# A hybrid decoder layer (differential attention and gated linear attention): the order of every engine's instructions made by a list scheduler over tiles

## The chip, the cores and the metric

The kernel runs on all 8 cores of one Trainium2 chip, each with one sequence of the batch. The time is that of the slowest core, in microseconds of the device. Executions come in two states. In the slow one the cores of one die (0 to 3 or 4 to 7) show a lower granted TensorE clock: in one execution of the kernel before, of 2403 us, cores 4 to 7 ran at 0.742 to 0.744 and cores 0 to 3 at 0.847 to 0.850. Names of engines in the profile: PE is TensorE's matmul, PEld its weight load, DVE is VectorE, ACT is ScalarE, POOL is GpSimd, SP is the queue that issues DMAs.

## The reference

Each sequence of 4096 tokens of width 1024 goes through this (cut to what matters):

```python
h = rms_norm(x, g_pre)
proj = h @ w_in                                   # (B, S, 5648)
qa, ka, va, za, qb, kb, vb, zb, lr, gate_a, gate_b = split(proj)
# mixer A: 4 heads, two score maps each, causal, ALiBi
pd = softmax(qa1 @ ka1.T * scale + bias) - lam * softmax(qa2 @ ka2.T * scale + bias)
oa = rms_norm(pd @ va, g_sub_a) * (1.0 - lam_init)
ya = (oa * silu(za)) @ w_up_a
# mixer B: gated linear attention (GLA), a chunked recurrence over the sequence
ob = rms_norm(gla_chunked(qb, kb, vb, glog), g_sub_b)
yb = (ob * silu(zb)) @ w_up_b
# merge, output projection, post-norm, residual
y = sigmoid(gate_a) * ya + sigmoid(gate_b) * yb
out = x + rms_norm(y @ w_out, g_post)
```

## The kernel before

A core works through 8 tiles of 512 tokens. Weights are converted to bf16 in the first tile, written to a scratch in HBM, and streamed from there in chunks of 1 MB for the later tiles. A small recorder collects operations with what they read and write. Each engine then runs its operations in the order written, with waits where data cross engines. The overlap of stages is therefore what the author wrote into the order by hand:

```python
        for t in range(ntiles):
            # [cut: norm of the first tile, first weight loads, debug stops]
            phase_b1(t)              # GLA projections
            gla_at(t, 0)
            gla_rest(t, 0)
            phase_b2(t)              # Q, K, V and silu(z_a) projections
            # [cut: the deferred pieces of GLA and of the norm of attention's output]
            for s in range(4):
                attention_jobs(t, s, deferred)
                # [cut: refill deferred]
            # [cut: load and statistics of the next tile's input]
            phase_e(t, lambda: attn_post(t))     # gates, up-projections, merge
            # [cut: hooks that put the next tile's norm between the steps of phase_f]
            phase_f(t, hooks)                    # output projection, post-norm, residual
```

Within attention, scores for one key block go out ahead of the value products of the block before, and pieces of GLA come in at four fixed places:

```python
        def attention_jobs(t, h, deferred):
            nkb = 4 * t + 4
            # [cut: emit_qk_pair issues two 64-row score matmuls of 512 queries, mask matmuls on
            #  the diagonal, and one exponential of 128x1024 on ScalarE; emit_pv issues up to four
            #  value products of 129 columns for one map]
            for kb in range(nkb + 1):
                if kb < nkb:
                    emit_qk_pair(kb)
                if kb >= 1:
                    emit_pv(kb - 1, 0)
                    emit_pv(kb - 1, 1)
                    r_done = (kb - 1) - 4 * t
                    if r_done >= 1:
                        attention_evac(t, h, r_done)
                # [cut: tile 0]
                else:
                    for f in deferred.get(kb, ()):
                        f()
```

In PSUM the program lays out 4 banks for projections and scores alike, 1 for transposes and 3 for the attention accumulators. The normalized input (hT), the queries, and the buffers of the merge exist once; several share memory (silu of z lies in the merge's output, the attention output's transpose in the queries).

Of the kernel before, what the change touches and what calls it, by code (L numbers as in the profile page):

```python
# [10 lines left out]
F32 = mybir.dt.float32  # L11
# [6 lines left out]
D = 1024  # L18
# [6 lines left out]
C_QA, C_KA, C_VA, C_ZA, C_QB, C_KB, C_VB, C_ZB, C_LR, C_GA, C_GB = 0, 512, 1024, 1536, 2048, 2304, 2560, 3072, 3584, 3600, 4624  # L25
CHUNK_COL = [C_QA, C_KA, C_VA, C_ZA, C_QB, C_VB, C_ZB, C_GA, C_GA + 512, C_GB, C_GB + 512]
CH_QA, CH_KA, CH_VA, CH_ZA, CH_QK, CH_VB, CH_ZB, CH_GA0, CH_GA1, CH_GB0, CH_GB1, CH_WO0, CH_WO1 = range(13)
NEG = -30000.0
NSLOT = 4

ENGS = ("pe", "act", "dve", "pool", "sp")

class _Op:
    __slots__ = ("eng", "fn", "deps", "is_dma", "sem", "val", "needs_inc")

    def __init__(self, eng, fn, is_dma):
        self.eng = eng
        self.fn = fn
        self.deps = []
        self.is_dma = is_dma  # L40
        self.sem = None
        self.val = 0
        self.needs_inc = is_dma

class _Prog:
    def __init__(self, same_eng_sync=("act", "dve", "pool")):
        self.ops = []
        self.last_writer = {}
        self.readers = {}
        self.same_eng_sync = set(same_eng_sync)  # L50
        self.dma_slots = []

    def op(self, eng, fn, reads=(), writes=(), dma=None):
        o = _Op(eng, fn, dma is not None)
        deps = {}
        for k in reads:
            w = self.last_writer.get(k)
            if w is not None:
                deps[id(w)] = w
        for k in writes:  # L60
            w = self.last_writer.get(k)
            if w is not None:
                deps[id(w)] = w
            for r in self.readers.get(k, ()):
                deps[id(r)] = r
        o.deps = list(deps.values())
        for k in reads:
            self.readers.setdefault(k, []).append(o)
        for k in writes:
            self.last_writer[k] = o  # L70
            self.readers[k] = []
        if dma is not None:
            o.sem = dma
            if dma not in self.dma_slots:
                self.dma_slots.append(dma)
        self.ops.append(o)
        return o

    def emit(self, block_engines, sems):
        ops = self.ops  # L80
        for o in ops:
            for d in o.deps:
                if d.is_dma:
                    continue
                if d.eng != o.eng or (d.eng in self.same_eng_sync):
                    d.needs_inc = True
        cnt = {e: 0 for e in ENGS}
        dcnt = {}
        for o in ops:
            if o.is_dma:  # L90
                slot = o.sem
                dcnt[slot] = dcnt.get(slot, 0) + 16
                o.sem = sems[slot]
                o.val = dcnt[slot]
            elif o.needs_inc:
                cnt[o.eng] += 1
                o.sem = sems[o.eng]
                o.val = cnt[o.eng]
        same = self.same_eng_sync

        def make(eng_name):
            my_ops = [o for o in ops if o.eng == eng_name]

            def body(e):
                waited = {}
                for o in my_ops:
                    need = {}
                    for d in o.deps:
                        if (not d.is_dma) and d.eng == eng_name and eng_name not in same:
                            continue  # L110
# [17 lines left out]
def _build(ntiles=NT, debug=False, stop_after=None):  # L128
    nc = bass.Bass("TRN2", target_bir_lowering=False)
# [6 lines left out]
    w_up_a = din("w_up_a", [512, D])  # L136
    w_up_b = din("w_up_b", [512, D])
# [7 lines left out]
    negm_d = din("negmask", [128, 128], BF16)  # L145
    btab_d = din("biastab", [128, 128])
    ef_d = din("eftab", [128, 4])
    rmask_d = din("resetmask", [128, 512], BF16)
    out = nc.dram_tensor("out", [S, D], F32, kind="ExternalOutput").ap()
    wsc = nc.dram_tensor("wsc", [13, 128, 4096], BF16).ap()  # L150
    dbg = {}
    if debug:
        for nm, shp in (("d_hT", [128, 8, 512]), ("d_QT", [128, 4, 512]), ("d_oacc", [128, 4, 4, 128]),
                        ("d_ob", [128, 4, 512]), ("d_yT", [128, 8, 512]), ("d_gaT", [128, 4, 512]),
                        ("d_gbT", [128, 4, 512]),
                        ("d_eb", [128, 2, 512]), ("d_state", [128, 2, 128])):
            dbg[nm] = nc.dram_tensor(nm, shp, F32, kind="ExternalOutput").ap()

    P = _Prog()
    with ExitStack() as es:  # L160
# [3 lines left out]
        def PSM(name, shape, dt):  # L164
# [3 lines left out]
        V = SB("V", [128, 4 * ntiles, 4, 130], BF16)  # L168
        wupA = SB("wupA", [128, 4, 1024], BF16)
        wupB = SB("wupB", [128, 4, 1024], BF16)  # L170
        wbuf = [SB(f"wbuf{i}", [128, 4096], BF16) for i in range(NSLOT)]
        wlr = SB("wlr", [128, 8, 16], BF16)
        walpha = SB("walpha", [16, 256], BF16)
        xn = [SB(f"xn{i}", [128, 1024], F32) for i in range(2)]
        xr = xn
        xa = [SB(f"xa{i}", [128, 1024], F32) for i in range(2)]
        hb = [SB(f"hb{i}", [128, 1024], BF16) for i in range(2)]
        hT = SB("hT", [128, 8, T], BF16)
        gated = [hb[i][:, 0:512] for i in range(2)]
        obf = [hb[i][:, 512:1024] for i in range(2)]  # L180
        QT = SB("QT", [128, 4, T], BF16)
        yT = SB("yT", [128, 8, T], BF16)
        szA = yT[:, 0:4, :]
        szB = yT[:, 4:8, :]
        gbT = SB("gbT", [128, 4, T], BF16)
        gl = SB("gl", [128, 2, T], F32)
        sq = gl[:, 0, :]
        lamv = gl[:, 0, 0:256]
        lamt = gl[:, 0, 256:384]
        wlr_st = gl[:, 1, 0:128].rearrange("p (kc c) -> p kc c", kc=8)  # L190
        cum = SB("cum", [128, 2, T], F32)
        walpha_st = cum[0:16, 0, 0:256]
        enb = cum
# [3 lines left out]
        vb = SB("vb", [128, 4, 512], BF16)  # L197
        lrT = SB("lrT", [16, T], BF16)
        state = SB("state", [128, 2, 128], F32)
        stbf = SB("stbf", [128, 2, 128], BF16)  # L200
        PT2 = [SB(f"PT{i}", [128, 2, 512], BF16) for i in range(2)]
        gatedA = SB("gatedA", [128, 4, 512], BF16)
        khT = gatedA[:, 0:2, :]
        oaf = [SB(f"oaf{i}", [128, 128], F32) for i in range(4)]
        junkb = SB("junkb", [128, 128], BF16)
        otmp = [SB(f"otmp{i}", [128, 128], F32) for i in range(2)]
        gaT = QT
        eb = SB("eb", [128, 2, T], F32)
        tga = [eb[:, 0, :], eb[:, 1, :]]
        ttmp = tga  # L210
        ztmp = [PT2[i][:].rearrange("p a b -> p (a b)").bitcast(F32) for i in range(2)]
        eblast = SB("eblast", [128, 2, 4], F32)
        tgb = [SB("tgb0", [128, 512], F32)] * 2
        ATs = [SB("ATs0", [128, 512], BF16)] * 2
        ident = SB("ident", [128, 128], BF16)
        tri4 = SB("tri4", [128, 512], BF16)
        negm = SB("negm", [128, 128], BF16)
        btab = SB("btab", [128, 128], F32)
        eft = SB("eft", [128, 4], F32)
        rmask = SB("rmask", [128, 512], BF16)  # L220
        gpost = SB("gpost", [128, D], F32)
        smalls = SB("smalls", [128, 12], F32)
        lams = SB("lams", [128, 8], F32)
        nbal = SB("nbal", [128, 2], F32)
        ss = SB("ss", [128, 32], F32)
        rs = SB("rs", [128, 32], F32)
        rstd = SB("rstd", [128, 32], F32)
        ssa = SB("ssa", [128, 16], F32)
        rsa = SB("rsa", [128, 16], F32)
        rstda = SB("rstda", [128, 16], F32)  # L230
        ssb = SB("ssb", [128, 16], F32)
        rsb = SB("rsb", [128, 16], F32)
        rstdb = SB("rstdb", [128, 16], F32)
        ssz = SB("ssz", [128, 64], F32)
        rsz = SB("rsz", [128, 32], F32)
        rstdz = SB("rstdz", [128, 32], F32)
        rz = SB("rz", [128, 8], F32)
        dbgbuf = SB("dbgbuf", [128, 8, 512], F32) if debug else None
        dbgoa = SB("dbgoa", [128, 4, 4, 128], F32) if debug else None
        pg4 = PSM("pg4", [128, 4, 512], F32)  # L240
        pg = [pg4[:, i, :] for i in range(4)]
        ptr = PSM("ptr", [128, 8, 128], BF16)
        poa = [PSM(f"poa{i}", [128, 512], F32) for i in range(3)]

        dma_names = (["stg%d" % i for i in range(8)] + ["wst%d" % i for i in range(NSLOT)] + ["wld%d" % i for i in range(NSLOT)]
                     + ["cst", "xn0", "xn1", "xr0", "xr1", "xa0", "xa1", "st0", "st1", "dbg"])
        sems = {}
        for nm in list(ENGS) + dma_names:
            sems[nm] = es.enter_context(nc.semaphore("s_" + nm))
        _build.sbuf_left = nc.sbuf_bytes_remaining  # L250
        block = es.enter_context(nc.Block())

        gctr = [0]

        def alloc_pg():
            b = gctr[0] % 4
            gctr[0] += 1
            return b

        def wkeys(slot):  # L260
            return [f"w{slot}_{i}" for i in range(8)]

        def ev_engine(i):
            return "dve"
# [87 lines left out]
        def emit_load():  # L352
            i = wstate["loaded"]
            if i >= len(wseq):
                return
# [661 lines left out]
```

## Time and profile before

| | before |
|---|---|
| median (3 fast runs) | 2246.97 us, 2242.42 the lowest |
| cores | 2225.9 to 2247.1 us, clock 0.842 to 0.851 |
| TensorE busy, idle (core 4) | 1704.0 us, 543 us |
| ScalarE, VectorE busy | 843.7 us, 934.1 us |
| granted clock (core 4) | 0.846 |

A row of the profile such as `L703 PE MATMUL ps_poa<-sb_V,sb_PT ... x4224 | 396.8, 244 | 123.3 <-ACT ...` reads: line of the program, engine, operation, written tile and read tiles, count, busy time in us, mean ns of one, idle time of the engine just before such instructions, and what ended it. In the rows of 40 slices each digit is tenths of a slice. The recorded lengths of successive matmuls overlap, so the mean of 393 ns for 512 columns is not their spacing, which is about 216 ns in dense stretches. The lines themselves are shown in the prediction.

### The profile page before, as it was taken

The numbers are of one execution on the slowest core, as the hardware profiler recorded it, in microseconds if no ns is written. First come the engines' busy times: TensorE is split into PE (matmuls) and PEld (weight loads), VectorE is DVE, ScalarE is ACT, GpSimd is POOL, SyncE is SP. The second block draws the span as 40 slices with busy tenths as digits, with TensorE's granted clock in tenths as the row PEclk, the third lists the DMA queues.
The fourth block names the chain that finished last, engine by engine and source line by source line (L and its number), as shares of the span: only waits on it lengthen the run. The fifth ranks groups of instructions, "written<-read, shape, count | busy, mean of one in ns | idle before, by whom it ended". The sixth has DMA issues, their size and how long they took to land.

```text
span 2247.1 us, 32959 instructions; the slowest of 8 cores (2225.9 to 2247.1 us)
## 1 busy us (share of the span) xinstructions
PE 1704.0 (76%) x10609; PEld 868.4 (39%) x10704; DVE 934.1 (42%) x2699; ACT 843.7 (38%) x1109; POOL 235.6 (10%) x438
## 2 busy tenths in 40 slices
PE   2554669787977877887878878778787878787786
PEld 1222324443444334443444434444334443344443
DVE  2446445544544454334523454323452234422324
ACT  2321221322144224523166232663316652256642
POOL 1002110111012001101001010010100010000100
PEclk9675789678977987798898988989898989899898
DMA  7992152104310341015300243000530003410002
GB/s 193 261 274 79 50 184 106 55 35 173 112 39 1 133 150 75 1 38 187 131 1 1 77 169 111 1 1 38 188 132 1 1 1 132 150 57 1 1 1 113
DMA packets 48615, 194.10 MB, mean 86 GB/s; under 512 B 6832, under 2 KB 7360, under 8 KB 35136
## 3 DMA queue, kind: packets, MB, share of 16 engines
q1 hardware_dynamic: 41968, 161.59, 21.6%
q0 software_dynamic: 6480, 30.41, 3.6%
q8 instruction: 89, 1.46, 0.3%
q14 instruction: 78, 0.64, 0.1%
HBM read 161.57 MB, written 30.41 MB: 85 GB/s over the span
## 4 chain that ended last, share of the span: by engine, by line
PE 55%; DVE 15%; ACT 9%; issue 9%; DMA 6%; POOL 4%; SPq 1%; DVEq 1%; ACTq 0%; POOLq 0%
PE ps_pg L399 16%; PE ps_pg L407 9%; PE ps_poa L703 9%; ACT sb_PT L694 8%; PE ps_pg L676 4%; DMA sb_KT<-w_in 3%; PE ps_pg L823 3%; PE ps_pg L831 3%; PE ps_pg L866 2%; POOL sb_rstda L772 2%; POOL sb_rstdb L429 2%; PE ps_poa L866 2%; DVE sb_junkb L765 2%; PE ps_pg L684 2%; PE ps_pg L688 2%
## 5 line engine op out<-in xcount | busy, mean ns | idle before, releaser
L694 ACT ACTIVATE sb_PT<-ps_pg 128x1024 bf16<-128x1024 f32 (+1 forms) x576 | 540.7, 953 | 428.3 <-PE ps_pg L676 238.6
L703 PE MATMUL ps_poa<-sb_V,sb_PT 128*128 128x129 bf16 x4224 | 396.8, 244 | 123.3 <-ACT sb_PT L694 93.4
L399 PE MATMUL ps_pg<-sb_hT,sb_wbuf 128*128 128x512 bf16 x1743 | 415.7, 393 | 20.6 <-ACT sb_eb L814 11.4
L703 PEld LDWEIGHTS ps_poa<-sb_V,sb_PT 128*128 128x128 bf16 x4224 | 291.2, 108 | 283.5 <-issue 277.7
L399 PEld LDWEIGHTS ps_pg<-sb_hT,sb_wbuf 128*128 128x128 bf16 x1792 | 180.4, 101 | 243.1 <-issue 52.4
L407 PE MATMUL ps_pg<-sb_wbuf,sb_hT 128*128 128x512 bf16 x994 | 239.4, 399 | 6.6 <-DVE sb_V L559 2.1
L676 PE MATMUL ps_pg<-sb_QT,sb_KT 64*128 64x512 bf16 x896 | 205.3, 448 | 21.0 <-DVE sb_yT L571 9.8
L731 DVE RECIPROCAL sb_rz<-ps_poa 128x3 f32<-128x3 f32 (+1 forms) x96 | 16.4, 171 | 481.5 <-PE ps_poa L703 481.5
L407 PEld LDWEIGHTS ps_pg<-sb_wbuf,sb_hT 128*128 128x128 bf16 x1024 | 103.8, 102 | 139.1 <-issue 36.5
L453 PE MATMUL ps_ptr<-sb_ident,sb_hb 128*128 128x128 bf16 x256 | 28.7, 281 | 129.0 <-DVE sb_hb L448 129.0
L814 ACT ACTIVATE sb_eb<-ps_pg 128x512 f32<-128x512 f32 x64 | 38.2, 597 | 234.2 <-PE ps_pg L399 234.2
L569 ACT ACTIVATE sb_PT<-ps_pg 128x512 f32<-128x512 f32 x32 | 19.0, 596 | 277.4 <-PE ps_pg L407 271.5
L826 DVE SCALAR_TENSOR_TENSOR sb_gl<-sb_eb,ps_pg 128x512 f32<-128x512 f32 x64 | 44.0, 688 | 177.2 <-PE ps_pg L823 163.9
L613 POOL CAST sb_stbf<-sb_state 128x128 bf16<-128x128 f32 x64 | 18.8, 294 | 888.5 <-PE ps_pg L597 694.9
L772 POOL TENSOR_TENSOR sb_rstda<-sb_rsa,sb_lams 128x1 f32<-128x1 f32 x128 | 69.7, 567 | 395.2 <-DVE sb_rsa L770 395.2
L645 PE MATMUL ps_ptr<-sb_ident,sb_hb 128*128 128x128 bf16 x128 | 18.0, 290 | 87.0 <-DVE sb_hb L636 87.0
L866 PE MATMUL ps_pg<-sb_wbuf,sb_yT 128*128 128x512 bf16 x320 | 76.1, 390 | 2.4 <-DVE sb_yT L837 2.4
L676 PEld LDWEIGHTS ps_pg<-sb_QT,sb_KT 64*128 64x128 bf16 x896 | 43.9, 95 | 85.6 <-issue 55.6
L453 PEld LDWEIGHTS ps_ptr<-sb_ident,sb_hb 128*128 128x128 bf16 x256 | 22.0, 126 | 139.3 <-issue 139.3
L823 PE MATMUL ps_pg<-sb_QT,sb_wupA 128*128 128x512 bf16 x248 | 70.7, 410 | 6.7 <-DVE sb_QT L789 6.3
L880 POOL TENSOR_TENSOR sb_rstdz<-sb_rsz,sb_lams 128x1 f32<-128x1 f32 x32 | 27.9, 873 | 429.6 <-DVE sb_rsz L878 429.6
L831 PE MATMUL ps_pg<-sb_gbT,sb_wupB 128*128 128x512 bf16 x256 | 72.2, 408 | 0.0
(116 smaller groups left out, 1932.2 us busy)
## 6 DMA issues: line engine op xcount, KB each, us to landing
sb_wbuf<-wsc SPq DMA_DIRECT2D x91, 1024.0 KB, 4.9
sb_KT<-w_in SPq DMA_DIRECT2D x88, 256.0 KB, 8.8
sb_xa<-x SPq DMA_DIRECT2D x32, 512.0 KB, 6.2
sb_xn<-x SPq DMA_DIRECT2D x32, 512.0 KB, 6.3
out<-sb_xn POOLq DMA_DIRECT2D x32, 512.0 KB, 5.4
wsc<-sb_wbuf POOLq DMA_DIRECT2D x13, 1024.0 KB, 9.9
sb_KT<-w_out SPq DMA_DIRECT2D x16, 256.0 KB, 8.5
sb_KT<-w_up_a SPq DMA_DIRECT2D x8, 256.0 KB, 10.0
```

The source lines that it names most:

```text
L399: P.op("pe", lambda e, lhsT=lhsT, kc=kc: e.matmul(out=pg[b][0:rows, :], lhsT=lhsT, rhs=hT[:, kc, :], start=(kc == 0), stop=(kc == 7)), rea ...
L407: P.op("pe", lambda e, kc=kc: e.matmul(out=pg[b][:, :], lhsT=hT[:, kc, s * 128:(s + 1) * 128], rhs=wbuf[slot][:, kc * 512:(kc + 1) * 512], ...
L429: P.op("pool", lambda e, q_=q_: e.tensor_tensor(out=dst[:, col0 + q_:col0 + q_ + 1], in0=src[:, col0 + q_:col0 + q_ + 1], in1=lams[:, 5:6] ...
L453: P.op("pe", lambda e, kc=kc: e.transpose(out=ptr[:, kc, :], in_=hb[i][:, kc * 128:(kc + 1) * 128], identity=ident[:]), reads=[f"hbL{i}", ...
L676: P.op("pe", lambda e, b=b, lhsT=lhsT, m=m: e.matmul(out=pg[b][:, :], lhsT=lhsT, rhs=QT[64 * m:64 * m + 64, h, :], start=True, stop=True), ...
L684: P.op("pe", lambda e, b=b: e.matmul(out=pg[b][:, c0:c0 + 128], lhsT=ident[:, :], rhs=negm[:, :], start=False, stop=True), reads=["ident", ...
L694: P.op("act", lambda e: e.activation(out=PT2[pp][:, :, c0:512], in_=pg4[:, bp:bp + 2, c0:512], func=AF.Exp, bias=cbias, scale=1.0), reads= ...
L703: P.op("pe", lambda e, a=a, i_=i_: e.matmul(out=acc_ap(m, a, 0, 129), lhsT=PT2[pp][:, m, a * 128:(a + 1) * 128], rhs=V[:, kb, h, 0:129], s ...
L772: P.op("pool", lambda e, ci=ci: e.tensor_tensor(out=rstda[:, ci:ci + 1], in0=rsa[:, ci:ci + 1], in1=lams[:, 5:6], op=ALU.pow), reads=[f"rs ...
L823: P.op("pe", lambda e, kc=kc, j=j, bya=bya: e.matmul(out=pg[bya][:, :], lhsT=wupA[:, kc, j * 128:(j + 1) * 128], rhs=gaT[:, kc, :], start= ...
L831: P.op("pe", lambda e, kc=kc, j=j, byb=byb: e.matmul(out=pg[byb][:, :], lhsT=wupB[:, kc, j * 128:(j + 1) * 128], rhs=gbT[:, kc, :], start= ...
L866: P.op("pe", lambda e, kc=kc, kk=kk, slw=slw, hh=hh, zb_=zb_: e.matmul(out=zb_, lhsT=yT[:, kc, s * 128:(s + 1) * 128], rhs=wbuf[slw][:, kk ...
```

## The change

The intent: at every moment, run on TensorE whatever is ready, from whichever stage and tile. The recorder becomes a list scheduler that runs when the program is built. Each operation carries an estimated cost and the engines that can do it (a copy may go to VectorE or ScalarE). The scheduler repeatedly places the operation that can start first; among equal starts, the one of the lower priority number, then the one written first. Buffers are given out from pools as operations are placed. The core of the diff (about 1,700 lines in all; cuts marked):

```diff
+SEM_LAT = 0.14
+ATT, PRE, GLA, FILL = 0, 1, 2, 3
...
+    def schedule(self):
...
+                for o in avail[e]:
+                    if e == "pe" and lock is not None and o.atom != lock:
+                        continue
+                    st = o.ready if o.ready > ef else ef
...
+                    key = (st, o.prio, o.idx)
+                    if best is None or key < best[:3]:
+                        best = (st, o.prio, o.idx, o, e)
...
-        hT = SB("hT", [128, 8, T], BF16)
+        hT = [SB(f"hT{i}", [128, 8, T], BF16) for i in range(2)]
+        QT = [SB(f"QT{i}", [128, 4, T], BF16) for i in range(2)]
...
-        pg4 = PSM("pg4", [128, 4, 512], F32)
-        ptr = PSM("ptr", [128, 8, 128], BF16)
-        poa = [PSM(f"poa{i}", [128, 512], F32) for i in range(3)]
+        qk = PSM("qk", [128, 4, 512], F32)
+        acc = [PSM(f"acc{i}", [128, 512], F32) for i in range(2)]
+        NPG = 2
+        pg = [PSM(f"pg{i}", [128, 512], F32) for i in range(NPG)]
...
+            nb = len(pairs) // 2
+            for b in range(nb + 1):
+                if b < nb:
+                    atom = (t, b)
+                    qk_pair(pairs[2 * b], 0, atom, pairs[2 * b + 1])
+                    qk_pair(pairs[2 * b + 1], 1, atom)
+                if b >= 1:
+                    pv_pair(pairs[2 * b - 2])
+                    pv_pair(pairs[2 * b - 1])
...
+        stage_batt([t for t in (0, 1) if t < ntiles])
+        for t in range(ntiles + 1):
+            P.prio = FILL
+            if t < ntiles:
+                stage_za(t)
+            if t > 0:
+                stage_e(t - 1)
+                stage_f(t - 1)
+            if t < ntiles:
+                stage_glaproj(t)
+                stage_gla(t)
+                stage_att(t)
+            if 1 <= t and t + 1 < ntiles:
+                stage_a(t + 1)
+                P.prio = FILL
+                stage_batt([t + 1])
```

`stage_a` is the norm, `stage_batt` the Q, K, V projections, `stage_za` the silu gate, `stage_e` the merge with its gates and up-projections, `stage_f` the output projection. Smaller changes come with it: score blocks are 256 queries by 256 keys and go out two at a time; the causal mask moves from matmuls to GpSimd (`affine_select`); the up-projection weights are streamed too, through 3 slots instead of 4; V is scaled in one instruction instead of four.

## The prediction

> **What bounds the kernel now.** I read first the page's busy totals and its rows of 40 slices (tenths of each slice; PEclk is the granted TensorE clock, also in tenths).
>
> ```profile
> PE 1704.0 (76%) x10609; PEld 868.4 (39%) x10704; DVE 934.1 (42%) x2699; ACT 843.7 (38%) x1109; POOL 235.6 (10%) x438
> ...
> PE   2554669787977877887878878778787878787786
> ...
> PEclk9675789678977987798898988989898989899898
> ```
>
> TensorE is by far the busiest, and no other engine passes 42%. It is neither full nor at full clock: 543 us of the 2247 are idle, and the mean clock is 0.846. All eight cores look alike (2225.9 to 2247.1 us), so this is no slow die.
>
> Second, busy time by stage for the last tile (start:end, length, busy us and instruction count of PE, PEld, DVE, ACT, POOL; then clock, DMA share, GB/s): norm and projections, attention, merge with output projection, tail.
>
> ```profile
> 1904.00:1981.00 77.00, 59.78 (x280) 27.37 (x284) 39.77 (x81) 17.08 (x27) 5.27 (x8) 0.89 0.43 157
> 1981.00:2173.00 192.00, 148.70 (x1365) 87.61 (x1364) 46.46 (x202) 125.71 (x131) 18.88 (x38) 0.89 0.02 7
> 2173.00:2228.00 55.00, 52.65 (x233) 23.74 (x239) 22.75 (x39) 12.49 (x26) 2.16 (x3) 0.94 0.15 58
> 2228.00:2247.00 19.00, 2.37 (x11) 0.88 (x9) 6.60 (x13) 1.38 (x4) 3.27 (x5) 0.67 0.44 166
> ```
>
> Each stage has its own limit. The merge stage is dense TensorE. Attention leaves TensorE 43 us idle and ScalarE 66 us. The norm of the next tile leaves TensorE 17 us idle. No stage lends its idle TensorE time to another.
>
> Third, the order in time inside attention (start, length, engine, line). The first three rows are from a stretch after a stall, the rest from the steady state.
>
> ```profile
> 2042.83 0.61 PE L676 MATMUL ps_pg<-sb_QT,sb_KT 64*128 64x512 bf16 x2
> ...
> 2043.38 1.05 PE L703 MATMUL ps_poa<-sb_V,sb_PT 128*128 128x129 bf16 x8
> ...
> 2044.35 0.61 PE L676 MATMUL ps_pg<-sb_QT,sb_KT 64*128 64x512 bf16 x2
> ...
> 2050.12 0.61 PE L703 MATMUL ps_poa<-sb_V,sb_PT 128*128 128x129 bf16 x8 [0.25 <-ACT sb_PT L694]
> 2050.66 0.10 PEld L676 LDWEIGHTS ps_pg<-sb_QT,sb_KT 64*128 64x128 bf16 x2
> 2050.66 0.39 PE L676 MATMUL ps_pg<-sb_QT,sb_KT 64*128 64x512 bf16 x2
> 2051.19 0.47 PEld L703 LDWEIGHTS ps_poa<-sb_V,sb_PT 128*128 128x128 bf16 x8 [0.43 <-issue]
> 2051.22 0.61 PE L703 MATMUL ps_poa<-sb_V,sb_PT 128*128 128x129 bf16 x8 [0.17 <-ACT sb_PT L694]
> 2051.24 2.12 ACT L694 ACTIVATE sb_PT<-ps_pg 128x1024 bf16<-128x1024 f32 x2 [0.16 <-PE ps_pg L676]
> ```
>
> Warm, one key block takes some 1.14 us (half of two) and the exponential sets it: 1.02 us each, 2.12 for two, plus a 0.16 wait; TensorE waits 0.2 us a block. Cold, the same block takes 1.52 us and TensorE sets it: the value products stretch from 0.61 to 1.05 us.
>
> Fourth, what TensorE waits for.
>
> ```profile
> PE ps_ptr L453 <- DVE sb_hb L448: 129.0, 32, 19.6
> PE ps_poa L703 <- ACT sb_PT L694: 93.4, 239, 11.2
> PE ps_ptr L645 <- DVE sb_hb L636: 87.0, 26, 8.0
> ```
>
> These are the norm of the next tile, the exponential, and the gated-linear-attention (GLA) output: all waits that other tiles' projections could fill.
>
> [...]in 5 us windows over all cores the clock reads 1.00 or 0.50 most often, 0.50 just after the stalls above (1915 to 1920)[...]. [...]from 2185 to 2195 us all eight cores are 99% busy at 1.00. [...]The 64-row pair ends 0.39 us after its start, of which 512 columns at the projection rate are 0.22; so about 0.17 us is a tail[...], by my reading. [...]The trace has 16 loads of 1283 ns: one more at the start, the rest at Ln and at the tanh after it.
>
> **The change, part by part.**
>
> 1. Order. Every engine's order is now made by a list scheduler at build time, with attention of tile t interleaved with merge and output of t-1, projections of t+1 and GLA. Doubled hT and QT, separate szA, szB, gatedA, gaT and gbT, four PT buffers, and PSUM split into 4 score banks, 2 accumulators and 2 for all else make it legal. It adds no work; it moves projections into the 543 idle us and keeps the clock up. So I add what TensorE must do at full clock:
> - Projections: 8 tiles x (44 groups x 8 + 8 low-rank + 64 up + 64 out) = 3904 matmuls of 512 columns. Dense runs take about 0.216 us each (46 to 47 per 10 us): 843 us. It stays.
> - Attention: still 4224 value products, and 544 score blocks of 256 queries x 256 keys in place of 576 of 512 x 128. Eight value products take 0.54 us start to next phase. The scores of two blocks now go out together: 2 x 0.22 + one 0.17 tail = 0.61, then 16 value products at about 1.00: 1.61 per two blocks; 272 x 1.61 = 438 us, less some 13 for shorter diagonals: 425.
> - The 256 mask matmuls (62 us busy) and the split score matmuls of the diagonal go; 64 masks on GpSimd of an estimated 0.65 us (the program's own figure) come, off TensorE and with spare time there (10% busy).
> - GLA: 32 steps x about 1.3 us (two 256-column pairs and eight 0.105 us products) = 41; 576 transposes at an estimated 0.07 = 40.
> Sum: 843 + 425 + 81 = 1349 us.
>
> 2. Start. Weights are still converted on chip. 15 chunks x (2 MB read + 1 MB written) = 45 MB, at the 240 to 280 GB/s of today's first 100 us, is some 170 us. Projecting Q, K and V for two tiles from one conversion gives TensorE about 120 to 135 us of work in that time, where before it was 181 us busy in the first 345. I charge 50 us.
>
> 3. Tail: the last tile's merge has nothing beside it but is dense already (52.65 of 55); after the last matmul 19 us are left: 19 us.
>
> 4. Streaming the up-projections too: 102 loads of 1 MB for 91, about 205 MB over 1500 us, 137 GB/s. A load lands in 4.9 us, three slots: hidden.
>
> 5. Losses. The other engines no longer have the idle time either: ScalarE carries 544 exponentials (480 x 1.02 + 64 x 0.81 = 543 us) and about 310 of tanh, squares, decay and some copies, 850 us; VectorE 850 to 930. In the last tile ScalarE needs 124 x 1.07 + 34 = 167 us beside 182 for TensorE, so a fixed order can't overlap them perfectly. Two PSUM banks for all projections: a silu group computes 1.73 us, then its bank is read by tanh (0.6) and VectorE (0.69), with waits 1.6 to 1.7: just balanced, and short when a 1.02 us exponential is ahead in the queue. I charge 9% of 1349, 120 us; this is judgment, not measured.
>
> Sum: 1349 + 50 + 19 + 120 = 1538, so **1540 us**.
>
> **Rivals.** (a) Two projection banks become the bound: GLA steps hold both for 3 to 4 us; 32 of these plus slow evictions would cost another 100 to 150 us: about 1670. For it: ten kinds of producers share two banks; against: attention has banks of its own to run meanwhile. [...](c) ScalarE becomes the bound in late tiles: 167 against 182 says no, and at worst adds 50 us. (d) Weight reloads stall behind stores and x loads in one in-order SP queue: 5 us each if exposed, but slots come free about one tile part ahead; small. (e) Ln sits between interleaved exponentials and tanhs and costs table loads: still one Ln per tile, so about 16 loads[...]. (f) Little gain, because time is only relabelled: refuted by the clock and idle numbers, as the work at full clock is 60% of the span.
>
> **Range and chances.** Low end: losses 30 us: 1450. High end: bank trouble[...]: 1720. Faster by over 2%: 0.97; within 2%: 0.02; slower: 0.01.
>
> **What would show it right or wrong.** PE busy at 85 to 92% of a span near 1540 with PEclk at 9 or more in almost all slices after the first five: order and clock right. Projection matmuls at about 0.216 us spacing: right[...]. Waits on TensorE for VectorE or ScalarE at projection groups, longest in total: rival (a). Exponentials back to back with little idle before them in the last tiles: rival (c). ACT table loads much above 16: rival (e). A first tile's clock of 0.5 past 200 us would break the start term.

## The result

The changed kernel takes 1670.09 us in the median (1668.22 to 1671.13, four runs, all fast) against 2246.97. The outputs are right. The ratio is 0.742 (95% interval 0.738 to 0.746). A ratio here is the mean time of one kernel's fast runs over that of the other's of the same rounds, so not quite the ratio of the medians. Executions in which one die ran at a lower clock are left out of the means. The time lies inside the forecast range, 130 us above the forecast figure.

The page of the changed kernel: busy totals, and the 40 slices of TensorE and of its clock.

```profile
PE 1423.9 (85%) x11082; PEld 753.7 (45%) x11280; DVE 737.7 (44%) x2214; ACT 913.8 (55%) x1232; POOL 252.8 (15%) x424
...
PE   2986865799878997799977999779999879999886
...
PEclk9998987799999998999989999989999979999798
```

The count x11082 is 198 short of the 11280 weight loads: some matmul records of this core are missing, so its busy time is too low and its idle time too high. Six of the eight cores have all their records; there TensorE is busy 1430 to 1435 us and idle 217 to 227. In the profile of the kernel before (95 records short on the core shown) the six complete cores are busy 1701 to 1712 us and idle 522 to 532.

So idle TensorE time fell by some 300 us and busy time by some 270; the mean clock of the slowest core went from 0.846 to 0.943. How the busy part divides can be estimated by weighting each 5 us window's busy time with its granted clock, on cores with all records. This is rough, since the recorded ends of matmuls are modelled. It gives 1495 us of work at full clock before (core 0) and 1382 after (core 3): some 113 us are fewer or shorter instructions, and some 160 us are the higher clock. But the rows are not full all the way: pairs of 7s return at even distances. The next view takes the span apart there (columns as in the prediction: start:end, length, busy us and count of PE, PEld, DVE, ACT, POOL, then clock, DMA share, GB/s).

```profile
520.00:640.00 120.00, 114.62 (x1016) 64.21 (x1032) 51.28 (x157) 73.61 (x90) 15.08 (x27) 1.00 0.26 90
640.00:720.00 80.00, 60.46 (x322) 27.65 (x329) 42.09 (x120) 32.35 (x55) 16.98 (x28) 0.89 0.39 143
720.00:840.00 120.00, 117.52 (x1132) 68.85 (x1152) 44.83 (x145) 81.06 (x96) 14.67 (x25) 1.00 0.23 80
840.00:920.00 80.00, 59.49 (x301) 26.61 (x306) 41.51 (x118) 30.61 (x52) 15.77 (x26) 0.88 0.45 158
...
1360.00:1555.00 195.00, 189.88 (x1890) 113.01 (x1922) 70.72 (x203) 140.41 (x171) 20.24 (x33) 0.99 0.26 93
```

Stretches of two kinds alternate. In the long ones TensorE is 96 to 98% busy at full clock. In the short ones it is 74 to 76% busy, the clock reads 0.88 to 0.89, and neither VectorE nor DMA is near full. What runs in them is seen from the exponentials of attention alone (busy us and count of ScalarE, clock, DMA):

```profile
640.00:680.00 40.00, 0.00 (x0) 0.87 0.54 194
680.00:720.00 40.00, 2.95 (x4) 0.91 0.24 93
720.00:760.00 40.00, 21.68 (x24) 1.00 0.23 80
760.00:800.00 40.00, 26.50 (x29) 1.00 0.23 81
```

The short stretches are those without attention. TensorE's order in time shows what is left there, the output projection (into ps_pg from sb_yT), the transposes of the next tile's norm (L450) and GLA's projections:

```profile
645.95 4.42 PE L446 MATMUL ps_pg<-sb_wbuf,sb_yT 128*128 128x512 bf16 x15 [0.22 <-issue]
650.80 3.61 PE L446 MATMUL ps_pg<-sb_wbuf,sb_yT 128*128 128x512 bf16 x16 [0.44 <-DVE sb_tmp L874]
655.54 1.89 PE L446 MATMUL ps_pg<-sb_wbuf,sb_yT 128*128 128x512 bf16 x8 [1.12 <-DVE sb_statA L572]
657.26 0.61 PE L450 MATMUL ps_pg<-sb_ident,sb_hb 128*128 128x128 bf16 x8
659.38 0.61 PE L450 MATMUL ps_pg<-sb_ident,sb_hb 128*128 128x128 bf16 x8 [1.51 <-ACT sb_hT L438]
661.17 1.00 PE L446 MATMUL ps_pg<-sb_wbuf,sb_yT 128*128 128x512 bf16 x3 [1.19 <-DVE sb_tmp L874]
```

The dense kind looks like this, a score atom of two blocks, value products and projections in turn without a gap:

```profile
1476.40 0.61 PE L755 MATMUL ps_qk<-sb_QT,sb_KT 64*128 64x256 bf16 x8
1476.94 0.63 PE L446 MATMUL ps_acc<-sb_V,sb_PT 128*128 128x129 bf16 x8
1477.62 0.81 PE L446 MATMUL ps_pg<-sb_hT,sb_wbuf 128*128 128x512 bf16 x3
1478.27 0.62 PE L446 MATMUL ps_acc<-sb_V,sb_PT 128*128 128x129 bf16 x8
1478.72 0.59 PE L446 MATMUL ps_pg<-sb_hT,sb_wbuf 128*128 128x512 bf16 x2
```

The ledger of idle TensorE time, from such stretches of the whole span:

| part of the span | us | idle TensorE us | clock |
|---|---|---|---|
| start, 0 to 320 | 320 | 96 | 0.92 |
| six stretches with attention, between 320 and 1555 | 840 | 25 | 0.96 to 1.00 |
| five stretches without it, between 440 and 1360 | 395 | 98 | 0.85 to 0.89 |
| after the last attention, 1555 to 1667 | 112 | 25 | 0.87 |

This is core 4, with its missing records. On core 3, which has all of them (span 1660.0 us), the idle time is 93 us in the first 320, 109 between 320 and 1555, and 25 after that.

### The profile page after: what moved, and what is told of

Read it like the earlier page. It is cut to its first block, busy times and chain, and to the rows that moved or that the text cites. A ratio compares the mean times of both kernels' runs of the same rounds, so it can differ in the third digit from the quotient of the medians.

```text
span 1667.4 us, 34067 instructions; the slowest of 8 cores (1647.5 to 1667.4 us)
## 1 busy us (share of the span) xinstructions
PE 1423.9 (85%) x11082; PEld 753.7 (45%) x11280; DVE 737.7 (44%) x2214; ACT 913.8 (55%) x1232; POOL 252.8 (15%) x424
## 4 chain that ended last, share of the span: by engine, by line
PE 73%; DVE 8%; issue 6%; DMA 5%; ACT 5%; POOL 1%; SPq 1%; DVEq 0%; ACTq 0%; POOLq 0%
PE ps_pg L446 48%; PE ps_acc L446 16%; PE ps_qk L755 8%; DMA sb_KT<-w_in 2%; PE ps_pg L450 1%; DMA sb_xa<-x 1%; DVE sb_gatedB L726 1%; DVE sb_xr L883 1%; DVE sb_tmp L874 1%; ACT sb_cum L438 1%; DMA sb_KT<-w_out 1%; DVE sb_szB L589 1%; SPq L504 1%; ACT sb_junk L871 1%; DVE sb_junkd L717 1%
## 5 line engine op out<-in xcount | busy, mean ns | idle before, releaser
L763 ACT ACTIVATE sb_PT<-ps_qk 128x1024 bf16<-128x1024 f32 (+1 forms) x544 | 514.4, 996 | 197.6 <-PE ps_qk L755 156.0
L446 PE MATMUL ps_acc<-sb_V,sb_PT 128*128 128x129 bf16 x4224 | 326.0, 220 | 10.3 <-POOL sb_PT L768 3.4
L446 PEld LDWEIGHTS ps_acc<-sb_V,sb_PT 128*128 128x128 bf16 x4224 | 258.4, 97 | 126.6 <-issue 99.9
L853 DVE SCALAR_TENSOR_TENSOR sb_tmp<-sb_tmp,ps_pg 128x512 f32<-128x512 f32 x128 | 87.8, 687 | 253.7 <-PE ps_pg L446 161.1
L755 PE MATMUL ps_qk<-sb_QT,sb_KT 64*128 64x256 bf16 (+1 forms) x2176 | 162.6, 268 | 1.6 <-ACT sb_PT L763 0.7
L838 ACT ACTIVATE sb_tmp<-ps_pg 128x512 f32<-128x512 f32 x128 | 76.8, 600 | 113.8 <-PE ps_pg L446 105.8
L755 PEld LDWEIGHTS ps_qk<-sb_QT,sb_KT 64*128 64x128 bf16 x2176 | 83.5, 94 | 105.1 <-issue 95.6
L807 POOL TENSOR_TENSOR sb_statE<-sb_statE,sb_mhalf 128x1 f32<-128x1 f32 x128 | 72.6, 581 | 268.9 <-DVE sb_statE L805 249.5
L588 ACT ACTIVATE sb_tmp<-ps_pg 128x512 f32<-128x512 f32 x64 | 38.3, 598 | 68.2 <-PE ps_pg L446 60.2
L450 PE MATMUL ps_pg<-sb_ident,sb_hb 128*128 128x128 bf16 x256 | 25.5, 260 | 57.2 <-DVE sb_hb L576 40.8
L446 PE MATMUL ps_pg<-sb_gaT,sb_wbuf 128*128 128x512 bf16 x252 | 69.9, 379 | 1.7 <-DVE sb_tmp L853 0.8
L446 PE MATMUL ps_pg<-sb_gbT,sb_wbuf 128*128 128x512 bf16 x229 | 65.5, 378 | 4.2 <-DVE sb_tmp L853 1.6
```

Source lines behind the costliest of these rows:

```text
L446: return P.op(_pe(n), lambda e: e.matmul(out=out_f(), lhsT=lf(), rhs=rf(), start=start, stop=stop, **kw), reads=reads, writes=writes, mode ...
L450: return P.op(_pe(128), lambda e: e.transpose(out=out_f(), in_=in_f(), identity=ident[:]), reads=list(reads) + ["ident"], writes=writes, m ...
L588: P.op({"act": _act(512, True)}, lambda e: e.activation(out=tmp[z.i][:], in_=pg[b.i][:], func=AF.Tanh, scale=0.5), reads=[b], writes=[z])
L755: lambda e, kb=kb, m=m, kbi=kbi, ca=ca, n=n: e.matmul(out=qk[:, 2 * half + m, kbi * 256:kbi * 256 + n], lhsT=KT[64 * m:64 * m + 64, h, kb ...
L763: P.op({"act": _act(2 * width, True)}, lambda e: e.activation(out=PT[pt.i][:, :, 0:width], in_=qk[:, 2 * half:2 * half + 2, 0:width], func ...
L807: P.op({"pool": (0.45, 0.1)}, lambda e: e.tensor_tensor(out=statE[st.i][:, 4:5], in0=statE[st.i][:, 3:4], in1=mhalf[:, 0:1], op=ALU.pow), ...
```

## The experiments

Theory A: the gain is the interleaving of stages, and the 130 us beyond the forecast figure come from the scheduler's priorities. Attention wins every tie, is used up early in each tile's turn, and leaves the rest of that turn (output projection, norm, GLA) to run alone, as short chains over two banks, at a clock of 0.85 to 0.89 on core 4. The rivals are named with each run. All ten kernels gave correct results. The runs were made on three chips; on these the fast runs of the kernel before agree within 0.3% in the median, so that times are compared directly.

### Everything in program order

Only the operation written next may be placed; costs, buffers and operations stay as in the changed kernel.

```diff
                 for o in avail[e]:
+                    if o.idx != len(order):
+                        continue
                     if e == "pe" and lock is not None and o.atom != lock:
```

> The changed kernel with its operations, buffers and costs unchanged, but the list scheduler may place an operation only when all operations written before it are placed, so that every engine runs in program order and no tile's projections go beside attention. Theory A (the gain is the interleaving of stages): at least as slow as the kernel before, 2200 to 2600 us, with TensorE idle more than 700 us and a mean clock under 0.87. Rival B (the gain is the smaller operations: score blocks in pairs, no mask matmuls, copies shared with ScalarE): stays under 1900 us.

Measured: 2701.44 us, ratio 1.201 to the kernel before. The page's totals:

```profile
PE 1664.3 (62%) x11280; PEld 882.4 (33%) x11280; DVE 755.5 (28%) x2146; ACT 967.8 (36%) x1301; POOL 239.6 (9%) x424
```

The time is even above the range given: the kernel before had overlap written in by hand, and this program order has none of that. The same matmuls that take 1430 to 1435 us in the changed kernel take 1664 here, at a mean clock of 0.80; weighted with the clock as above they are 1400 us, so that most of the difference is the clock. TensorE is idle for 1029 us (2693.6 - 1664.3). Rival B, that the smaller operations carry the gain, falls: the same operations without the order are slower than before. The order is worth 1031 us against program order; against the order made by hand the whole change is worth 577. The smaller changes (the mask, V in one instruction, the streamed up-projections) were not taken back one by one.

### Attention at the priority of the filling work

```diff
-ATT, PRE, GLA, FILL = 0, 1, 2, 3
+ATT, PRE, GLA, FILL = 2, 0, 1, 2
```

> One line: attention has the same priority as the filling projections in the scheduler's ties, so program order decides. Theory A (the 130 us lost beyond the forecast lie in seven stretches of some 80 us between two attentions in which no attention is left to run, because attention wins every tie and is used up early): exponentials appear in these stretches, TensorE is busy over 90% in the middle tiles instead of 73 to 75% there, the clock is over 0.96 in them, and the time falls to 1570 to 1630 us; the last tile's attention is then left alone and gives part back. Rival B (two projection banks are the bound whatever the order): within 1.5% of 1670 us.

Measured: 1604.71 us, ratio 0.713, 65 us below the changed kernel, within theory A's range and outside rival B's. From 320 to 1400 us of the profiled run TensorE is busy 1022.31 us of 1080 (95%) at a clock of 0.99, as theory A said. (The expectation speaks of seven stretches; the ledger counts five long ones, with shorter ones at the start and the end.) The cost that was foreseen is there as well: from 1400 to 1480 us of this kernel's profiled run TensorE is 81% busy (64.58 of 80) and from 1480 to 1520 only 73% (29.22 of 40), with 347 matmuls, because the last tile's attention runs alone: in the second stretch no projection is left.

One thing is not separated. The edit also puts the next tile's norm (PRE) and GLA ahead of attention, where they came after it. Whether attention's tie with the filling work or this earlier norm and GLA gives the gain, no run tests; both are the order.

### The same, but attention first in the last tile

```diff
-            P.prio = ATT
+            P.prio = ATT if t < 7 else 0
```

> As the equal-priority kernel, but in the last tile attention again goes first. Theory A: the last attention no longer runs alone; 30 to 60 us below the equal-priority kernel, 1530 to 1580 us. Rival B: no change from 1670 us. Rival C (ScalarE is the bound in the last tile): no better than the equal-priority kernel.

Measured: two fast runs of five, 1562.24 and 1563.52 us. That is 107 us below the changed kernel and 42 below the run before; it rests on two runs, but the best version below holds the gain in nine fast ones. First the same view of the exponentials as in the result, now of this kernel, then the page's slices:

```profile
640.00:680.00 40.00, 20.91 (x22) 1.00 0.21 73
680.00:720.00 40.00, 7.75 (x8) 1.00 0.41 152
720.00:760.00 40.00, 10.99 (x12) 0.96 0.43 159
760.00:800.00 40.00, 10.95 (x12) 1.00 0.56 172
```

```profile
PE 1387.9 (89%) x11280; PEld 759.2 (49%) x11280; DVE 753.5 (48%) x2248; ACT 883.7 (57%) x1198; POOL 246.4 (16%) x424
...
PE   1987865799999999899889999999998998999986
...
PEclk9999987889999999999999999999999999999998
```

Between 320 us and the end of the last attention at 1480, no 20 us are without exponentials now, and the pairs of 7s after the start are gone. This core has all its records: TensorE idles 173 us (1560.6 - 1387.9) instead of 217 to 227, and the same matmuls take some 45 us less of busy time, at a clock of 0.977. Theory A holds in this: the same two banks, buffers and operations, in another order, take 107 us less. Rival C falls too, since giving the last attention its priority back gains time.

### One score block at a time

```diff
-            nb = len(pairs) // 2
-            for b in range(nb + 1):
-                if b < nb:
-                    atom = (t, b)
-                    qk_pair(pairs[2 * b], 0, atom, pairs[2 * b + 1])
-                    qk_pair(pairs[2 * b + 1], 1, atom)
-                if b >= 1:
-                    pv_pair(pairs[2 * b - 2])
-                    pv_pair(pairs[2 * b - 1])
+            for b in range(len(pairs) + 1):
+                if b < len(pairs):
+                    qk_pair(pairs[b], b % 2, (t, b))
+                if b >= 1:
+                    pv_pair(pairs[b - 1])
```

The extra dependency that tied the two halves of the score banks together goes with it (not shown).

> The changed kernel with scores issued one block at a time instead of two, so 544 changes into the 64-row mode and back instead of 272. My step says a change there and back costs about 0.2 us of TensorE[...]: 272 x 0.2 = 54 us more, 1715 to 1740 us. Rival[...]: under 1690 us.

Measured: 1737.71 us, ratio 0.772. That is 67.6 us for 272 more changes to the 64-row score matmuls and back, or 0.25 us each (67.6 / 272), near the 0.2 of the expectation. In this run's timeline the next matmul starts 0.33 us after a single block (1502.44 to 1502.77, 1503.09 to 1503.42), in the changed kernel's 0.54 us after a pair (1476.40 to 1476.94), so that two single blocks take 0.12 us more than a pair. Weighted with the clock, TensorE's work rises from 1382 to 1436 us on cores with all records, 0.20 us a change (an estimate); the rest is idle time and clock. Issuing two blocks together is thus a real part of the change, worth some 4%. Whether all of it is the change itself, or some of it the shorter run-ahead of the scores, this run does not separate.

### A shorter hold of the bank in the output projection

The bank was read by ScalarE (square, 598 ns) and then by VectorE (gain, 689 ns). Now one copy empties it, and both read the copy.

```diff
+ act: tmp = Copy(pg)                        # the only read of the bank
- act: Square(pg), summed into statF
- dve: tmp = pg * gpost
+ act: Square(tmp), summed into statF
+ dve: tmp = tmp * gpost
```

> The changed kernel, but the output projection's bank is emptied by one ScalarE copy; the square and the multiplication by the gain then read the copy. The bank is held some 0.8 us after a group instead of some 1.6. If the long hold of two banks is what starves TensorE in the stretches without attention (rival: banks): the output-projection part of each stretch, some 24 us for 13.8 us of matmuls, shrinks by 6 us or more, 7 times, 1615 to 1635 us. If the stretches suffer mainly from having nothing else to run, so that each short chain shows: 1640 to 1665 us.

Measured: 1645.17 us, ratio 0.730, 25 us below the changed kernel, at the border of the two expectations. So the hold of the two banks does cost time in the stretches without attention; it is not most of what they lose. Its meaning becomes clear in the last run.

### Raw weights loaded ahead of a free slot

```diff
-                 writes=[b], dma=lambda: f"stg{b.i}", nbytes=262144, claim=[w])
+                 writes=[b], dma=lambda: f"stg{b.i}", nbytes=262144)
```

> The changed kernel, but the load of a raw weight piece no longer waits until the converted chunk has a slot; it needs only a staging buffer, so the next chunk's pieces load while all three slots are in use. Tests the term for the start: if the first 320 us lose time because loading starts only when a slot comes free (waits of 16.7 us on the conversions, 57 us of the DMA queue on them), 12 to 30 us less, 1640 to 1658 us; if the start is bound by DMA bandwidth alone: within 5 us of 1670.

Measured: 1655.29 us, ratio 0.735, 15 us below the changed kernel. In the first 320 us TensorE is busy 239 to 242 us on the cores with all records, instead of 227 to 232. Loading that waits for a slot is a part of the start's loss, but of some 90 idle us it accounts for about 10. The longest wait that is left there is for the normalized input (28.5 us in four waits, the longest 16.9); the one on the conversions fell from 16.7 to 7.1 us. Whether the DMA rate lies behind the rest is not separated.

### A third buffer for the normalized input, and its control

The first edit gives hT three buffers and lets the norm of tile t wait for the gates of tile t-3 rather than t-2. To make room, the residual buffer and the gated GLA buffer go from two to one. The control makes only these two cuts.

```diff
-        hT = [SB(f"hT{i}", [128, 8, T], BF16) for i in range(2)]
+        hT = [SB(f"hT{i}", [128, 8, T], BF16) for i in range(3)]
-                     reads=[f"gates{t - 2}"] if t >= 2 else [])
+                     reads=[f"gates{t - 3}"] if t >= 3 else [])
-("xr", 2) ... ("gatedB", 2)
+("xr", 1) ... ("gatedB", 1)
```

> The changed kernel with three buffers for the normalized input instead of two, so that the norm of the next tile no longer waits for the merge gates of the tile before last; residual and gated-GLA buffers cut from two to one to make room. Rival theory (the two buffers are what keeps the next attention from starting): below 1620 us. Theory A (attention is used up early by its priority, whatever buffers there are): 1660 to 1710 us, the cut buffers costing a little.

> Control for the third input buffer: the changed kernel with one residual buffer and one gated-GLA buffer instead of two, and nothing else. If the third buffer in itself does nothing: within 1% of the 1691 us measured with it. If the third buffer helps and the cut hides it: 1720 us or more.

Measured: 1691.49 us (ratio 0.751) with the third buffer and 1689.95 (0.751) with the cuts alone. The third buffer does nothing, and the whole loss of 20 us against the changed kernel is that of the cuts. So the lifetime of hT, which on paper keeps the next tile's norm waiting, is not what leaves the stretches without attention as long as the priorities use attention up early. With the repaired priorities a third buffer was not tried.

### The best version

Equal priority except in the last tile, with the early loads of raw weights.

> Equal priority except in the last tile, with the early loads of raw weight pieces. If both effects are real and apart: 1535 to 1555 us fast, below the 1562 us of the same kernel without the early loads.

Measured: 1548.31 us (1546.93 to 1552.08), ratio 0.688 with an interval of 0.686 to 0.689. This beats both kernels, by 31% and 7%. The early loads again gain about 14 us.

Last, the short hold on top of it, with the edit shown above.

> Equal priority except in the last tile, early loads of raw pieces, and the short hold of the bank in the output projection. In the changed kernel the short hold gave 25 us in stretches in which nothing else ran. If it only shortened chains that showed for want of other work, it gives little where attention now fills them: 1538 to 1552 us against 1548. If two banks bind in their own right, it gives its 20 to 25 us again: under 1530 us.

Measured: 1547.64 us, ratio 0.689 (0.688 to 0.690). What gave 25 us in the changed kernel gives nothing here. The two banks bound the output projection only where it ran alone; with attention beside it, TensorE has other work while a bank is being emptied. For the output projection two banks were a cost because of the order, not in their own right. The other users of the banks (gates, GLA) had no such run.

## Why the prediction was right, point by point

- **What bounds the kernel.** Right. Filling the waits and keeping the clock up took out some 300 us of idle and 270 us of busy time, of which by the estimate above some 160 are the clock. In 5 us windows of the kernel before (all cores, from 100 us on, the tail left out) the mean clock is 0.72 where TensorE is busy for less than half of the window, 0.83 where it is busy for 50 to 90%, and 0.91 above that; in the changed kernel it is 0.79, 0.89 and 0.99. The clock shows again in the program-order run: 1664 us busy for an estimated 1400 us at full clock, at a mean clock of 0.80.
- **Work at full clock, 1349 us.** Near. On cores with all records the changed kernel's work, weighted with the clock, is 1382 us, 33 more; where these 33 are was not found. In the best version the same work is 1386 to 1390 us busy at a clock of 0.98. The cycle of two score blocks is close to its step: scores 0.54 us from start to the next phase against 0.61, value products 0.45 to 0.68 for eight against 0.50. (The prediction reads 0.54 for eight value products and then sums sixteen at 1.00.)
- **Mask to GpSimd.** Right: 64 masks of 655 ns against the estimated 0.65 us. TensorE waits 3.4 us for them in all.
- **Start, 50 us.** Too small: 88 to 93 us are idle in the first 320 on the cores with all records. Early loads brought back about 15 us of the whole time.
- **Tail, 19 us.** Near in sum: the last matmul of the changed kernel ends near 1659 of 1667 us, so 8 us follow it, and the stretch after the last attention loses 25 us in all.
- **Streaming hidden.** Right on the whole: 102 loads of 1 MB landing in 5.0 us, one wait of 3.1 us on them in TensorE's list.
- **Losses of 9%, 120 us.** As idle time this was about right, 109 us between 320 and 1555 on core 3, but the lower clock of the stretches with these losses (0.85 to 0.89 on core 4) was left out, and the sign "PEclk at 9 or more in almost all slices after the first five" failed in 9 of 35 slices. The cause of the losses was also not the one given. It was neither an imperfect overlap with ScalarE in the last tiles (TensorE was 97% busy there, 189.88 of 195 us) nor two banks in themselves, but the priorities that use attention up: another order gained 107 us.
- **The sum, 1538 us.** On core 3 the time of 1660 us is 1433 busy and 227 idle, against 1349 and 189 in the forecast. Of the 122 us between, an estimated 51 are the clock, 33 the work at full clock, 43 the start and 6 the end, less 11 in the middle. The 107 us that another order gained are not the same us: the repair left the start as it was (94 us idle) and cut the idle time of the middle to 61 us, well below the charge. That the best version, at 1548 us, lies near 1540 is thus partly a balance of a start charged too low and a middle charged too high.
- **Rivals.** (a) was half right, as shown by the short hold: 25 us with the old order, none with the new. Its figure, about 1670, was the author's estimate and is the measured one, but by luck: with the same two banks another order takes 107 us less. A lower clock under denser TensorE work does not show in the fast runs: from 1360 to 1555 us all eight cores of the changed kernel are 97 to 99% busy at 0.99 to 1.00, and the eight cores of the best version's profiled run have mean clocks of 0.978 to 0.984 over some 1540 us. The slow state took three of five runs of the equal-but-last kernel (0.842 to 0.925 on the cores of the slow die, 0.976 to 0.980 on the others); its cause was not looked into. (c), ScalarE, is refuted by the equal-but-last run. (e): the table loads of 1283 ns stay at 16 (8 before tanh, 7 before Ln, one at the start). (d) is small in the changed kernel, by the wait above. (f) is refuted by the result. The sum of the exponentials is 541 us, not 543; 514 were measured.

## What to carry to other kernels

A scheduler that prefers one stage in every tie can use up the very work that would have filled the others' waits; look for evenly spaced dips of TensorE and of its clock, and ask which stage is missing there. Before adding a buffer or shortening a hold, try the order: here a change of priorities gained 107 us, a third buffer nothing under the old priorities, and a shorter hold gained only until the order was right. When work is summed at full clock, a forecast needs a term for the clock too: the stretches with TensorE 73 to 80% busy ran at 0.85 to 0.89, and in all the lower clock cost an estimated 51 us beside 227 us of idle time.
